# A planned one-layer kernel: new costs in the model of time of its planner, and a bound on how early a load is issued

## The chip, the cores and the metric

The kernel runs on one core of a Trainium2 chip. The metric is the device time of one execution in microseconds (us). The kernel before took 2209.79 us, the median of three runs that lie between 2207.43 and 2212.3. The execution that the profiler recorded took 2211.71 us; its span, from the first instruction to the last, is 2209.6 us.

The engines are PE (matrix multiplications), DVE, ACT and POOL (element by element) and SP, which here issues nearly all the DMAs. Each engine works through its own list of instructions in order.

## The reference

One layer of a streaming encoder, in fp32, for 1024 rows of width 1024 and 256 memory rows. Cut to what matters:

```python
h = rmsnorm(x, norm_mix_g)
p = h @ w_in                      # q, k, v, z, decay, beta | q, k, v, r, low-rank gate | two merge gates
# branch A, 8 heads of 128: gated delta rule in chunks of 64 rows
lower = where(strict, beta * (k k^T) * decay, 0)
sol = triangular_solve(I + lower, [beta * v, beta * exp(gc) * k])     # then a scan over the chunks
# branch B, 4 heads: gated linear attention (GLA) in chunks of 64 rows
x += merge(sigmoid gates, branch A @ w_bgdn, branch B @ w_bgla) @ w_out
x += cross_attention(rmsnorm(x), rmsnorm(mem))      # 4 heads over the 256 memory rows
x += w2 @ relu(w1 @ rmsnorm(x)) ** 2                # d_ff = 4096
out = rmsnorm(x)                                    # the final norm
```

## The kernel before

**The work.** All large products are done as three fp32r matmuls of split operands (mm3, L518): high by high (L525), high by low (L527), low by high (L529). A split (L563 to L566) is a copy by ACT, which gives the high part, and a subtraction by DVE or POOL, which gives the low part. Most products of 1024 by 1024 are further cut by a scheme of seven block products; its operands, in slots named A0a to B1b, are sums of blocks that are loaded (tiles e, raw, rawa), added and split.

**The stages**, in the order in which the program is written: a first phase that projects the memory's keys (units K0 to K3, 48 matmuls of 128x256 each) and folds them into the query weights (units Q0 to Q3, fold_q, results stored through the tile gst, L731), the same for the values (V0 to V3) and output weights (O0 to O3), and normalises x beside it; the gates (g0 to g3, the first users of the normalised x); GLA; the gated delta rule (GDN), four pairs of heads with a block inverse each; the merge; the output projection; attention; the MLP; the last norm. The weight loads of the first phase are named raw, two loads of 512 KB for a unit. In the names of the orders below, raw_389 and raw_395 are the two halves of K2's weights, raw_468 and raw_474 of K3's, raw_539 and raw_545 of Q0's. x comes in two halves of 512 rows (x_553, x_1044), each by four loads of 512 KB. x_norm (L747 to L758) sums the squares (L630 to L634 with colsum L608), takes a reciprocal root (L556 to L560), spreads it over the partitions by PE (L622), multiplies (L755) and splits the result (L758, L566) into the slots A0a to A1b. t_sums (L798 to L801) then forms block sums of x in place.

**GDN's inverse.** For a pair of heads, gdn_subst (L1262) solves blocks of 32 rows by a chain of 31 steps, a product (L1283) and a sum (L1285) each, between two STREAM_TRANSPOSE (L1276, L1289); gdn_inverse (L1309, L1318) combines the blocks by matmuls that need the chain's result (PF). The next heads' masks are made by gdn_decay (load L1194, then L1195 to L1203).

**What sets the order.** A class, Plan, records the whole program once, gives each instruction a cost and a latency (Op, L72), derives the dependences, and then makes each engine's list anew. latest (L276) goes backwards and gives each instruction the latest start at which PE still keeps its times. forward (L303) then simulates the engines: whenever one is free, it takes the ready instruction with the earliest latest start. In it "ring" is the DMA engines taken together, "port" a resource that DVE and POOL share, and work marked flex may go to either of them. Four rounds of this are made, and the best one's lists are what the program issues. So a changed cost can move instructions anywhere.

Of the kernel before, what the change touches and what calls it, by code (L numbers as in the profile page):

```python
# [13 lines left out]
AF = mybir.ActivationFunctionType  # L14
# [46 lines left out]
ENGINES = {mybir.EngineType.PE: "tensor", mybir.EngineType.DVE: "vector", mybir.EngineType.Activation: "scalar",  # L61
           mybir.EngineType.Pool: "gpsimd", mybir.EngineType.SP: "sync"}
GATES = (0, 1, 2, 3)
ROUNDS, TOP, PAD, WINDOW = 4, 228656, 128, 3413


def size(ap):
# [6 lines left out]
class Op:  # L74


    dma = port = False
    bytes = 0

    def __init__(self, ins, flex):  # L80
        eng = self.eng = ENGINES[ins.engine]
        ins_, outs = [[x for x in q if getattr(x, "bass_ap", None) is not None] for q in (ins.ins, ins.outs)]
        n = size(outs[0])
        psum = lambda x: x.bass_ap.tensor.name[:3] in ("pd_", "ps_")
        self.name, self.opcode, self.acc = ins.name, ins.opcode, []
        for w, q in enumerate((ins_, outs)):
            for x in q:
                p = x.ap[0][0]
                lows, span = [x.bass_ap.offset % p if p > 1 else x.bass_ap.offset], 0
                for st, k in sorted(x.ap[1:]):  # L90
                    if st <= span + 1 or k * len(lows) > 16:
                        span += st * (k - 1)
                    else:
                        lows = [lo + st * i for lo in lows for i in range(k)]
                for lo in lows:
                    self.acc.append((x.bass_ap.tensor.name,) + ((0, HALF) if psum(x) else (lo, lo + span)) + (w,))
        sums = ins.opcode == "TensorTensor"
        two = sum(size(x) > 1 and not psum(x) for x in ins_) > 1
        self.flex = flex and sums and two and n > 16
        scalar = n > 1 and any(size(x) == 1 for x in ins_)  # L100
        far = [x for x in ins_ + outs if not psum(x) and x.ap[-1][0] * 4 > 64]

        scan = 118 * (getattr(ins, "is_tensor_tensor_scan", None) or False)
        times = {"vector": (150 + scan + n * 1.042 + 60 * scalar, 85, 34, 35), "gpsimd": (290 + n * 1.98 if sums else 160 + n * 0.9, 45, 60, 35)}
        if sums and n <= 16:
            times["gpsimd"] = 430 + n * 152, 45, 60, 35
        if ins.opcode == "TensorReduce":
            times["vector"] = 420, 85, 34, 35
        if ins.opcode == "StreamTranspose":
            times["vector"] = 1880 if far else 1245, 85, 34, 35  # L110
        if ins.opcode == "Memset" and far:
            times["gpsimd"] = 450, 45, 60, 35
        self.times = {e: (d - early, early + own, early + lat) for e, (d, early, own, lat) in times.items()}
        if ins.opcode == "DMACopy":
            self.dma, self.cost, self.own, self.lat = True, 60, 2600, 2600
            self.bytes = n * 4 * outs[0].ap[0][1]
        elif eng == "tensor":
            m = size(ins_[0])
            if ins.is_transpose:
                self.cost = m * 0.85  # L120
            elif ins_[0].dtype == F32R:
                self.cost = m * 0.4463 + (4 if m < HALF else 0)
            elif m == 64:
                self.cost = 59
            else:
                self.cost = max(m, size(ins_[1])) * 1.667 + 8
            self.own, self.lat = 0, 203
        elif eng == "scalar":
            d = (150 if psum(ins_[0]) else 190) + n * 0.84 + 90 * scalar + n * 0.9 * bool(far)
            self.cost, self.own, self.lat = d - 100 + 240 * (len(outs) > 1), 130, 135  # L130
        else:
            self.port = eng == "gpsimd" or n > 16 and not any(psum(x) for x in ins_ + outs)
            self.take(eng)

    def take(self, eng):
# [9 lines left out]

class Mark:

    eng, port, dma, flex, acc, cost, lat, opcode, bytes = "mark", False, False, False, (), 0, 0, "", 0

    def to(self, other, raw):  # L150
        return 0
# [5 lines left out]
class Plan:  # L157
# [119 lines left out]
    def latest(self, deps, at, end):  # L277

        ops, n = self.ops, len(self.ops)
        last = [end] * n  # L280
        users, order = [0] * n, []
        for d in deps:
            for j in d:
                users[j] += 1
        todo = [i for i in range(n) if not users[i]]
        while todo:
            i = todo.pop()
            o = ops[i]
            s = last[i] = at[i] if o.eng == "tensor" else last[i] - o.cost
            for j in deps[i]:  # L290
                q = ops[j]
                if q.eng != "tensor":
                    last[j] = min(last[j], s - q.to(o, j in self.raw[i]) - q.bytes / 300)
                users[j] -= 1
                if not users[j]:
                    todo.append(j)
        return last

    def forward(self, deps, prio):


        ops, n = self.ops, len(self.ops)
# [7 lines left out]
        ready, start, work = [0.0] * n, [0.0] * n, defaultdict(float)  # L310
        engs = ("vector", "scalar", "gpsimd", "sync", "tensor")
        now_q = {e: [] for e in engs + ("flex",)}
        wait_q = {e: [] for e in engs + ("flex",)}
        free = dict.fromkeys(engs + ("port", "ring"), 0.0)
        order = {e: [] for e in engs}
        events = [0.0]

        def arrive(i):
            if ops[i].eng == "mark":
                start[i] = ready[i]  # L320
                return done(after[i], ready[i], None)
            heapq.heappush(wait_q["flex" if ops[i].flex else ops[i].eng], (ready[i], i))
            heapq.heappush(events, ready[i])

        def done(us, e, i):
            for u in us:
                ready[u] = max(ready[u], e + (0 if i is None else ops[i].to(ops[u], i in self.raw[u])))
                left[u] -= 1
                if not left[u]:
                    arrive(u)  # L330

        def run(i, t):
            o = ops[i]
            if o.port:
                t = max(t, free["port"])
                free["port"] = t + o.cost
            start[i], e = t, t + o.cost
            if o.eng == "tensor":

                k = int(t / WINDOW)  # L340
                if k and work[k - 1] < 0.4 * WINDOW:
                    e += o.cost
                work[k] += e - t
            free[o.eng] = e
            order[o.eng].append(i)
            heapq.heappush(events, e)
            if o.dma:
                e = free["ring"] = max(e, free["ring"]) + o.bytes / 300
            done(users[i], e, i)
            done(after[i], t, None)  # L350

# [24 lines left out]
        while events:  # L376
# [3 lines left out]
            for e in ("flex",) + engs:  # L380
                w = wait_q[e]
                while w and w[0][0] <= now:
                    i = heapq.heappop(w)[1]
                    heapq.heappush(now_q[e], (i if e == "tensor" else prio[i], i))
            for e in engs:
                if free[e] <= now:
                    i = take(e, now)
# [1988 lines left out]
```

## Time and profile before

| what | us |
|---|---|
| median of three runs | 2209.79 |
| lowest and highest run | 2207.43, 2212.3 |
| profiled execution | 2211.71 |
| its span | 2209.6 |
| PE busy in it | 2156.5 |
| DVE busy | 1702.4 |
| ACT busy | 1094.8 |
| POOL busy | 203.9 |

The mean granted clock of PE over the span is 0.991 of full speed. In the rows below, a stretch such as 21.40:47.40 is given in us from the span's start; "x127" counts instructions; the clock is the mean share of full speed that PE was granted in the stretch. Matmuls overlap, so their pitch (start to start) is shorter than the time of one. A wait "A <- B" means that A's engine stood idle until B ended.

### The profile page before, as it was taken

The page shows a single profiled execution, that of the slowest core. Times are in us where ns is not written, and L with a number is a line of the kernel's source. Part 1 is how long each engine was busy: PE and PEld are TensorE (multiplying, and loading weights), DVE is VectorE, ACT ScalarE, POOL GpSimd, SP SyncE. Part 2 cuts the span into 40 slices and gives each one's busy share as a digit, 9 for nine tenths or more (in the row PEclk, how much of TensorE's full clock was granted, in tenths as well). Part 3 has the DMA queues.
Part 4 walks back from the last instruction along what each step waited for, and adds up shares of the span by engine and source line. Part 5 has one row for each costly group of instructions (what it writes and reads, how often), then busy time and mean ns, then how long its engine had stood idle before and what let it go on. Part 6 is the DMA issues. An engine that isn't in the chain of part 4 may idle for free.

```text
span 2209.6 us, 32225 instructions
## 1 busy us (share of the span) xinstructions
PE 2156.5 (98%) x11504; PEld 1838.5 (83%) x11504; DVE 1702.4 (77%) x3167; ACT 1094.8 (50%) x2215; POOL 203.9 (9%) x236
## 2 busy tenths in 40 slices
PE   7999999999999999999999999999999999999996
PEld 7888988988888888888877888998788888888886
DVE  8935997878796887969769984569989778567756
ACT  6444555354454635555445343465665556544433
POOL 1100000000131321313010000000100000000001
PEclk8999999999999999999999999999999999999998
DMA  6942122221310211202077761345464446778742
GB/s 232 305 162 77 59 92 71 80 72 58 120 59 29 74 47 44 77 20 72 30 267 272 247 211 56 110 126 160 127 208 140 160 148 209 243 251 273 245 122 81
DMA packets 147312, 300.21 MB, mean 136 GB/s; under 512 B 15688, under 2 KB 22216, under 8 KB 147152
## 3 DMA queue, kind: packets, MB, share of 16 engines
q1 hardware_dynamic: 140352, 289.75, 39.7%
q10 hardware_dynamic: 6800, 8.42, 1.1%
q8 instruction: 90, 1.47, 0.3%
q14 instruction: 70, 0.57, 0.1%
HBM read 212.35 MB, written 85.75 MB: 135 GB/s over the span
## 4 chain that ended last, share of the span: by engine, by line
PE 77%; DVE 11%; DMA 4%; issue 2%; ACT 1%; POOL 0%; SPq 0%; DVEq 0%; POOLq 0%; ACTq 0%
PE pd L529 18%; PE pd L525 18%; PE pd L527 18%; PE ps L529 4%; PE ps L525 4%; PE ps L527 4%; PE ps L1318 1%; PE ps L597 1%; DVE wop L566 1%; DMA e<-obd 1%; PE ps L1309 1%; DVE pr L1283 1%; DVE Pm L1285 1%; DMA A0b<-tgd 1%; PE ps L1358 1%
## 5 line engine op out<-in xcount | busy, mean ns | idle before, releaser
L565 ACT ACTIVATE wop<-raw 128x512 fp32r<-128x512 f32 (+1 forms) x472 | 314.7, 672 | 496.2 <-PE pd L529 234.5
L566 DVE TENSOR_TENSOR wop<-raw,wop 128x512 fp32r<-128x512 f32 (+1 forms) x434 | 309.2, 715 | 133.3 <-ACT wop L565 126.9
L1176 DVE SCALAR_TENSOR_TENSOR acc<-pd,convw,acc 128x511 f32<-128x511 f32 x144 | 106.7, 741 | 19.3 <-ACT acc L1173 18.8
L529 PE MATMUL pd<-t,wop 128*128 128x512 f32 x268 | 107.7, 402 | 0.0
L525 PE MATMUL pd<-t,wop 128*128 128x512 f32 x268 | 105.8, 395 | 0.1
L527 PE MATMUL pd<-t,wop 128*128 128x512 f32 x268 | 105.3, 393 | 0.1
L525 PE MATMUL pd<-B1a,wop 128*128 128x512 f32 (+1 forms) x220 | 82.4, 375 | 0.3 <-ACT B1a L565 0.3
L529 PE MATMUL pd<-B1a,wop 128*128 128x512 f32 (+1 forms) x220 | 82.3, 374 | 0.0
L529 PE MATMUL pd<-A1a,wop 128*128 128x512 f32 x180 | 72.3, 402 | 0.0
L527 PE MATMUL pd<-A1a,wop 128*128 128x512 f32 x180 | 70.8, 393 | 0.6 <-DVE A1a L566 0.6
L525 PE MATMUL pd<-A1a,wop 128*128 128x512 f32 x180 | 70.9, 394 | 0.0
L527 PE MATMUL pd<-B0b,wop 128*128 128x512 f32 x172 | 67.0, 390 | 0.0
L565 ACT ACTIVATE whi<-raw 128x512 fp32r<-128x512 f32 x70 | 41.9, 625 | 38.7 <-PE pd L527 29.2
L527 PEld LDWEIGHTS pd<-t,wop 128*128 128x128 f32 x268 | 50.3, 188 | 12.2 <-DVE t L566 0.6
L529 PEld LDWEIGHTS pd<-t,wop 128*128 128x128 f32 x268 | 50.4, 188 | 11.7
L525 PEld LDWEIGHTS pd<-t,wop 128*128 128x128 f32 x268 | 50.4, 188 | 11.3 <-ACT t L565 0.5
L527 PE MATMUL pd<-B1a,wop 128*128 128x512 f32 (+1 forms) x156 | 57.5, 369 | 0.0
L529 PE MATMUL pd<-A1b,wop 128*128 128x512 f32 x144 | 56.9, 395 | 0.0
L525 PE MATMUL pd<-A1b,wop 128*128 128x512 f32 x144 | 56.9, 395 | 0.0
L525 PE MATMUL pd<-A0a,whi 128*128 128x512 f32 x140 | 55.8, 399 | 1.0 <-ACT whi L565 1.0
L527 PE MATMUL pd<-A1b,wop 128*128 128x512 f32 x144 | 56.4, 392 | 0.0
L529 PE MATMUL pd<-A0b,wlo 128*128 128x512 f32 x140 | 56.5, 403 | 0.0
(600 smaller groups left out, 6991.3 us busy)
## 6 DMA issues: line engine op xcount, KB each, us to landing
raw<-in_w_dram SPq DMA_DIRECT2D x120, 256.0 KB, 3.7
raw<-in_w_gdn_dram SPq DMA_DIRECT2D x64, 256.0 KB, 3.0
raw<-in_w_dram SPq DMA_DIRECT2D x32, 512.0 KB, 3.9
e<-ad SPq DMA_DIRECT2D x63, 256.0 KB, 4.8
ad<-q SPq DMA_DIRECT2D x45, 256.0 KB, 3.1
rawa<-ad SPq DMA_DIRECT2D x42, 256.0 KB, 4.8
A0b<-tgd SPq DMA_DIRECT2D x32, 256.0 KB, 5.0
ad<-acc SPq DMA_DIRECT2D x30, 256.0 KB, 2.4
```

Of the source, the lines that this page charges most:

```text
L525: nc.tensor.matmul(out, lh, rh, start=first and i == 0, stop=False)
L527: nc.tensor.matmul(out, lh, rl, start=False, stop=False)
L529: nc.tensor.matmul(out, ll, rh, start=False, stop=last and i == n - 1)
L565: nc.scalar.activation(hi, raw, AF.Copy)
L566: (lo_eng or nc.gpsimd).tensor_tensor(lo, raw, hi.bitcast(F32), SUB)
L597: self.nc.tensor.transpose(pt[:, i * P:(i + 1) * P], s, self.ident)
L1176: nc.vector.scalar_tensor_tensor(x, pt[:, 0:HALF - d], tap, x, MUL, ADD)
L1283: nc.vector.tensor_tensor(pr, X[:, c + 1:32, c:c + 1].broadcast_to([P, m, n]), Pm[:, c:c + 1, 0:n].broadcast_to([P, m, n]), MUL)
L1285: nc.vector.tensor_tensor(Pm[:, c + 1:32, 0:n], Pm[:, c + 1:32, 0:n], pr, ADD)
L1309: nc.tensor.matmul(pt[:, i * 96:(i + 1) * 96], NT[:, u + i, :], PF[:, v + i, 0:96], start=True, stop=True)
L1318: nc.tensor.matmul(pt[0:96, i * n:(i + 1) * n], PF[:, v + i, 0:96], Z, start=True, stop=True)
L1358: nc.tensor.matmul(py[:, 0:P], st["NT"][:, c, :], zh[h], start=True, stop=True)
```

## The change

The planner's numbers are changed, and one rule is added. A DMA is taken to need 2050 ns instead of 2600 ns beside its transfer, and the DMA engines to move 390 instead of 300 bytes in a ns. A matmul of 64 columns costs 80 instead of 59. A row sum (accum_out) by ACT from SBUF costs 385 instead of 240. ACT pays 1283 when the table of functions changes (Ln on one side, Exp and Tanh on the other). The shared port is also taken by small operations with two SBUF inputs. The rule: a DMA that writes a tile on the chip is not ready before 30,000 ns ahead of its latest start.

```diff
@@ -61,7 +61,7 @@
 ENGINES = {mybir.EngineType.PE: "tensor", mybir.EngineType.DVE: "vector", mybir.EngineType.Activation: "scalar",
            mybir.EngineType.Pool: "gpsimd", mybir.EngineType.SP: "sync"}
 GATES = (0, 1, 2, 3)
-ROUNDS, TOP, PAD, WINDOW = 4, 228656, 128, 3413
+ROUNDS, TOP, PAD, WINDOW, LOAD, HORIZON = 4, 228656, 128, 3413, 1283, 30000
 
 
 def size(ap):
@@ -75,6 +75,7 @@
 
 
     dma = port = False
+    table = 0
     bytes = 0
 
     def __init__(self, ins, flex):
@@ -112,7 +113,7 @@
             times["gpsimd"] = 450, 45, 60, 35
         self.times = {e: (d - early, early + own, early + lat) for e, (d, early, own, lat) in times.items()}
         if ins.opcode == "DMACopy":
-            self.dma, self.cost, self.own, self.lat = True, 60, 2600, 2600
+            self.dma, self.cost, self.own, self.lat = True, 60, 2050, 2050
             self.bytes = n * 4 * outs[0].ap[0][1]
         elif eng == "tensor":
             m = size(ins_[0])
@@ -121,15 +122,16 @@
             elif ins_[0].dtype == F32R:
                 self.cost = m * 0.4463 + (4 if m < HALF else 0)
             elif m == 64:
-                self.cost = 59
+                self.cost = 80
             else:
                 self.cost = max(m, size(ins_[1])) * 1.667 + 8
             self.own, self.lat = 0, 203
         elif eng == "scalar":
             d = (150 if psum(ins_[0]) else 190) + n * 0.84 + 90 * scalar + n * 0.9 * bool(far)
-            self.cost, self.own, self.lat = d - 100 + 240 * (len(outs) > 1), 130, 135
+            self.cost, self.own, self.lat = d - 100 + (240 if psum(ins_[0]) else 385) * (len(outs) > 1), 130, 135
+            self.table = {AF.Ln: 1, AF.Exp: 2, AF.Tanh: 2}.get(ins.func, 0)
         else:
-            self.port = eng == "gpsimd" or n > 16 and not any(psum(x) for x in ins_ + outs)
+            self.port = eng == "gpsimd" or (n > 16 or two) and not any(psum(x) for x in ins_ + outs)
             self.take(eng)
 
     def take(self, eng):
@@ -145,7 +147,7 @@
 
 class Mark:
 
-    eng, port, dma, flex, acc, cost, lat, opcode, bytes = "mark", False, False, False, (), 0, 0, "", 0
+    eng, port, dma, flex, acc, cost, lat, opcode, bytes, table = "mark", False, False, False, (), 0, 0, "", 0, 0
 
     def to(self, other, raw):
         return 0
@@ -290,7 +292,7 @@
             for j in deps[i]:
                 q = ops[j]
                 if q.eng != "tensor":
-                    last[j] = min(last[j], s - q.to(o, j in self.raw[i]) - q.bytes / 300)
+                    last[j] = min(last[j], s - q.to(o, j in self.raw[i]) - q.bytes / 390)
                 users[j] -= 1
                 if not users[j]:
                     todo.append(j)
@@ -311,7 +313,7 @@
         engs = ("vector", "scalar", "gpsimd", "sync", "tensor")
         now_q = {e: [] for e in engs + ("flex",)}
         wait_q = {e: [] for e in engs + ("flex",)}
-        free = dict.fromkeys(engs + ("port", "ring"), 0.0)
+        free = dict.fromkeys(engs + ("port", "ring", "table"), 0.0)
         order = {e: [] for e in engs}
         events = [0.0]
 
@@ -319,6 +321,9 @@
             if ops[i].eng == "mark":
                 start[i] = ready[i]
                 return done(after[i], ready[i], None)
+            if ops[i].dma and any(w and t in self.tiles for t, _, _, w in ops[i].acc):
+
+                ready[i] = max(ready[i], prio[i] - HORIZON)
             heapq.heappush(wait_q["flex" if ops[i].flex else ops[i].eng], (ready[i], i))
             heapq.heappush(events, ready[i])
 
@@ -334,6 +339,10 @@
             if o.port:
                 t = max(t, free["port"])
                 free["port"] = t + o.cost
+            if o.table:
+
+                t += LOAD * (o.table != free["table"])
+                free["table"] = o.table
             start[i], e = t, t + o.cost
             if o.eng == "tensor":
 
@@ -345,7 +354,7 @@
             order[o.eng].append(i)
             heapq.heappush(events, e)
             if o.dma:
-                e = free["ring"] = max(e, free["ring"]) + o.bytes / 300
+                e = free["ring"] = max(e, free["ring"]) + o.bytes / 390
             done(users[i], e, i)
             done(after[i], t, None)
```

The instructions are the same on SP and PE; their places differ, and some of the flex work changes its engine. From this line on, line numbers of the changed kernel are 9 higher than those of the kernel before (L494 is L503 there).

SP's list at the start, before (x_553 and x_1044 are the halves of x; raw_389 and raw_395 K2's weights):

```order
9 L494 DMA raw_323<-in_wk_dram 128x1024
10 L494 DMA raw_329<-in_wk_dram 128x1024
11 L494 DMA x_553<-in_xT_dram 128x2x512 x4
12 L494 DMA x_1044<-in_xT_dram 128x2x512 x4
13 L663 DMA convw_184<-in_convw_dram 128x96
14 L494 DMA raw_389<-in_wk_dram 128x1024
15 L494 DMA raw_395<-in_wk_dram 128x1024
16 L494 DMA raw_468<-in_wk_dram 128x1024
17 L494 DMA raw_474<-in_wk_dram 128x1024
18 L494 DMA raw_539<-in_wqT_dram 128x2x512
```

SP's list at the start, now:

```order
9 L503 DMA raw_323<-in_wk_dram 128x1024
10 L503 DMA raw_329<-in_wk_dram 128x1024
11 L503 DMA x_553<-in_xT_dram 128x2x512
12 L503 DMA raw_389<-in_wk_dram 128x1024
13 L503 DMA x_553<-in_xT_dram 128x2x512 x2
14 L503 DMA raw_395<-in_wk_dram 128x1024
15 L503 DMA x_553<-in_xT_dram 128x2x512
16 L503 DMA raw_468<-in_wk_dram 128x1024
17 L503 DMA raw_474<-in_wk_dram 128x1024
18 L503 DMA raw_539<-in_wqT_dram 128x2x512
...
30 L503 DMA raw_1055<-in_wv_dram 128x1024
31 L503 DMA x_1044<-in_xT_dram 128x2x512 x3
32 L503 DMA raw_1061<-in_wv_dram 128x1024
33 L503 DMA x_1044<-in_xT_dram 128x2x512
```

One load of x stands ahead of K2's first weight half and three ahead of its second; the loads of the second half of x stand behind those of Q0 to O0.

PE's list after K1, before (pd_336 is K1's second result, pd_401 K2's; ps tiles are the sums of squares and the spread roots of mem and x):

```order
97 L529 MATMUL pd_336<-mT_206,wlo_331 128x256
98 L622 MATMUL ps_480<-ident_171,rs_o_418 128x128 x2
99 L608 MATMUL ps_971<-ones_178,acc_704 128x1 x4
100 L622 MATMUL ps_1014<-ident_171,rs_o_980 128x128 x4
101 L608 MATMUL ps_1331<-ones_178,acc_1121 128x1 x2
102 L525 MATMUL pd_401<-mT_206,wop_390 128x256
103 L527 MATMUL pd_401<-mT_206,wop_390 128x256
104 L525 MATMUL pd_402<-mT_206,wop_390 128x256
105 L527 MATMUL pd_402<-mT_206,wop_390 128x256
```

PE's list after K1, now:

```order
96 L538 MATMUL pd_336<-mT_206,wlo_331 128x256
97 L534 MATMUL pd_401<-mT_206,wop_390 128x256
98 L536 MATMUL pd_401<-mT_206,wop_390 128x256
99 L538 MATMUL pd_401<-mT_206,wlo_391 128x256
100 L534 MATMUL pd_401<-mT_206,wop_390 128x256
101 L536 MATMUL pd_401<-mT_206,wop_390 128x256
102 L538 MATMUL pd_401<-mT_206,wlo_391 128x256
103 L534 MATMUL pd_401<-mT_206,wop_390 128x256
104 L536 MATMUL pd_401<-mT_206,wop_390 128x256
105 L617 MATMUL ps_411<-ones_178,acc_300 128x1 x2
106 L538 MATMUL pd_401<-mT_206,wlo_391 128x256
```

K1's last matmul is followed by K2's first; the memory's sum (ps_411) comes within K2. The sums and roots of x come in Q3, O0 and V3.

DVE's list in the second of GDN's substitutions, before (L1283 and L1285 are the chain, gl, kf and dm the next heads' masks, acc the convolution):

```order
1022 L1283 TENSOR_TENSOR pr_7303<-X_7274,Pm_7276 128x207
1023 L1185 SCALAR_TENSOR_TENSOR acc_7454<-tg_7496,acc_7454 128x512
1024 L1285 TENSOR_TENSOR Pm_7276<-Pm_7276,pr_7303 128x23x9
1025 L1195 COPY gl_7963<-dm_7961 128x8
1026 L1283 TENSOR_TENSOR pr_7306<-X_7274,Pm_7276 128x220
1027 L1202 TENSOR_TENSOR kf_7971<-gl_7963,tm_186 128x8
1028 L1285 TENSOR_TENSOR Pm_7276<-Pm_7276,pr_7306 128x22x10
...
1056 L1179 SCALAR_TENSOR_TENSOR acc_7618<-last_7619,convw_184,acc_7618 128x3
1057 L1198 TENSOR_TENSOR dm_7975<-dm_7975,tm_186 128x1024
1058 L1285 TENSOR_TENSOR Pm_7276<-Pm_7276,pr_7330 128x14x18
```

DVE's list at the same steps of the chain, now:

```order
1032 L1292 TENSOR_TENSOR pr_7306<-X_7274,Pm_7276 128x220
1033 L1294 TENSOR_TENSOR Pm_7276<-Pm_7276,pr_7306 128x22x10
1034 L1194 SCALAR_TENSOR_TENSOR acc_7618<-tg_7657,acc_7618 128x512
1035 L1292 TENSOR_TENSOR pr_7309<-X_7274,Pm_7276 128x231
1036 L1269 TENSOR_SCALAR eq_7616<-ssq_7589 128x8
1037 L1294 TENSOR_TENSOR Pm_7276<-Pm_7276,pr_7309 128x21x11
1038 L1292 TENSOR_TENSOR pr_7312<-X_7274,Pm_7276 128x240
1039 L1294 TENSOR_TENSOR Pm_7276<-Pm_7276,pr_7312 128x20x12
1040 L1292 TENSOR_TENSOR pr_7315<-X_7274,Pm_7276 128x247
...
1057 L1294 TENSOR_TENSOR Pm_7276<-Pm_7276,pr_7330 128x14x18
1058 L1292 TENSOR_TENSOR pr_7333<-X_7274,Pm_7276 128x247
```

L1195, L1198 and L1202 no longer stand between the steps; they come later, outside the substitution.

SP's list in the merge, before (obd and tgd are results of the branches in memory, A0a here a residual from xT):

```order
268 L494 DMA e_11364<-obd_71 128x512
269 L494 DMA e_11368<-obd_71 128x512
270 L494 DMA A0a_12276<-in_xT_dram 128x2x512 x4
271 L494 DMA A0b_11580<-tgd_109 128x512
272 L494 DMA A0b_11580<-tgd_108 128x512
273 L494 DMA A0b_11580<-tgd_110 128x512 x2
274 L494 DMA A0b_11580<-tgd_108 128x512
275 L494 DMA A0b_11580<-tgd_111 128x512
276 L494 DMA A0b_11580<-tgd_109 128x512
...
279 L494 DMA e_11372<-obd_71 128x512
280 L494 DMA rawa_11534<-obd_73 128x512
281 L494 DMA rawa_11538<-obd_73 128x512
```

SP's list in the merge, now:

```order
273 L503 DMA e_11372<-obd_71 128x512
...
275 L503 DMA e_11376<-obd_72 128x512
276 L503 DMA e_11381<-obd_72 128x512
277 L503 DMA rawa_11534<-obd_73 128x512
278 L503 DMA rawa_11538<-obd_73 128x512
...
280 L503 DMA e_11385<-obd_72 128x512
281 L503 DMA e_11389<-obd_72 128x512
282 L503 DMA e_11529<-obd_73 128x512
283 L503 DMA rawa_11555<-obd_74 128x512
284 L503 DMA rawa_11559<-obd_74 128x512
285 L503 DMA e_11542<-obd_73 128x512
...
296 L503 DMA A0b_11580<-tgd_109 128x512
```

The obd loads stand together and the A0b loads behind them; the four xT loads come at 413 to 427 of the list.

## Rows read from the trace of the kernel before

**Rows 1.** The page, part 1: engine, busy us (share of the span), xinstructions.

```profile
PE 2156.5 (98%) x11504; PEld 1838.5 (83%) x11504; DVE 1702.4 (77%) x3167; ACT 1094.8 (50%) x2215; POOL 203.9 (9%) x236
```

**Rows 2.** Windows: stretch, length, busy us (xinstructions) by engine, granted clock, DMA share, GB/s.

```profile
21.40:47.40 26.00, 19.28 (x127) 19.00 (x127) 21.60 (x35) 18.00 (x30) 8.27 (x6) 0.74 0.53 185
47.40:78.70 31.30, 25.30 (x202) 24.03 (x201) 29.06 (x51) 13.35 (x17) 4.41 (x3) 1.00 0.78 246
78.70:130.30 51.60, 51.58 (x313) 45.06 (x314) 37.91 (x52) 29.46 (x42) 2.21 (x1) 1.00 0.92 314
...
552.40:1104.80 552.40, 542.09 (x3190) 471.53 (x3188) 443.50 (x1050) 280.61 (x797) 126.30 (x167) 0.99 0.18 57
1104.80:1215.30 110.50, 105.86 (x484) 84.57 (x483) 89.39 (x154) 54.55 (x108) 6.79 (x4) 1.00 0.78 269
```

**Rows 3.** Waits of PE: what waited, releaser, us in total, times, longest.

```profile
PE ps L1309 <- ACT PF L1295: 6.4, 3, 2.6
PE pd L525 <- DVE gst L731: 5.3, 4, 1.7
...
PE ps L1309 <- issue: 2.8, 1, 2.8
PE ps L525 <- ACT B1b L565: 2.8, 3, 1.4
```

**Rows 4.** Timeline of PE: start, us, instruction, idle before it and releaser.

```profile
30.05 2.08 PE L622 MATMUL ps<-ident,rs_o 128*128 128x128 f32 x8 [4.20 <-DVE rs_o L560]
...
47.25 0.28 PE L529 MATMUL pd<-mT,wlo 128*128 128x256 f32 x1
47.37 0.28 PE L525 MATMUL pd<-kv,wop 128*128 128x256 f32 x1
```

**Rows 5.** DMA, 0 to 36 us: rate by slice, issues, us to landing.

```profile
GB/s 0 0 130 341 314 328 266 325 241 314 394 337 416 394 394 403 396 385 389 387 389 385 391 378 391 377 405 397 423 387 382 118 32 0 0 0 0 0 0 46
...
x<-in_xT_dram SPq DMA_DIRECT2D x8, 512.0 KB, 9.4
raw<-in_wk_dram SPq DMA_DIRECT2D x6, 512.0 KB, 10.3
```

**Rows 6.** Timeline of ACT: the copy of K2's first weight half.

```profile
27.59 1.04 ACT L565 ACTIVATE wop<-raw 128x1024 fp32r<-128x1024 f32 x1
```

**Rows 7.** Groups of DVE instructions by form, 21.4 to 78.7 us.

```profile
L566 DVE TENSOR_TENSOR wlo<-raw,wop 128x1024 fp32r<-128x1024 f32 x13 | 18.0, 1385 | 2.0 <-PE pd L529 1.7 <-issue 0.2
L755 DVE SCALAR_TENSOR_TENSOR x<-x,cols,ps 128x512 f32<-128x512 f32 x14 | 9.9, 736 | 0.8 <-PE ps L622 0.8
L731 DVE TENSOR_TENSOR gst<-pd,rmb 128x256 f32<-128x256 f32 x26 | 9.6, 413 | 1.8 <-DMA Gd<-gst 1.7
L634 DVE TENSOR_TENSOR acc<-acc,sq 128x512 f32<-128x512 f32 x11 | 7.6, 692 | 0.6
```

**Rows 8.** Groups of POOL instructions by form, 6.5 to 80 us.

```profile
L566 POOL TENSOR_TENSOR A1a<-x,A1a 128x512 fp32r<-128x512 f32 x2 | 3.5, 1748 | 7.0 <-ACT A1a L565 7.0
```

**Rows 9.** Groups of DVE instructions by form, 78.7 to 130.3 us.

```profile
L798 DVE TENSOR_TENSOR x<-x 128x512 f32<-128x512 f32 x4 | 2.6, 686 | 0.0
```

**Rows 10.** Timeline of PE around 130 us: first use of row half 1.

```profile
130.26 0.40 PE L525 MATMUL pd<-A1b,wop 128*128 128x512 f32 x1
```

**Rows 11.** Timeline of PE in GDN, the first inverse.

```profile
674.12 6.89 PE L1309 MATMUL ps<-PF,NT 128*128 128x96 f32 x32 [2.82 <-issue]
```

**Rows 12.** Groups of DVE instructions in GDN, 631 to 672 us.

```profile
L1176 DVE SCALAR_TENSOR_TENSOR acc<-pd,convw,acc 128x511 f32<-128x511 f32 (+2 forms) x9 | 6.7, 741 | 0.6 <-ACT acc L1173 0.6
```

**Rows 13.** DMA of 1104.8 to 1165 us: issues, KB each, median us to landing.

```profile
e<-obd SPq DMA_DIRECT2D x18, 256.0 KB, 5.1
...
A0a<-in_xT_dram SPq DMA_DIRECT2D x4, 512.0 KB, 9.1
```

**Rows 14.** The page, part 6: DMA issues, KB each, median us to landing.

```profile
e<-ad SPq DMA_DIRECT2D x63, 256.0 KB, 4.8
...
rawa<-ad SPq DMA_DIRECT2D x42, 256.0 KB, 4.8
```

## The prediction

> **What bounds the kernel now.** I read the busy shares first, then the stretches, PE's waits, and the timeline inside the stretches that lose time. PE is busy 2156.5 of 2209.6 us [rows 1], so a change that issues the same instructions can win only where PE stands still or runs slowly. Three places do so. From 21.4 to 47.4 us PE is busy 19.28 of 26.00 us at a mean granted clock of 0.74, from 47.4 to 78.7 us 25.30 of 31.30; in GDN 10.3 of 552.4 us are idle, in the merge 4.6 of 110.5 [rows 2]. The longest waits belong to the same places: L1309 waits for the block inverses, fold_q for gst, the merge's matmuls for split operands [rows 3]. In the rest of the span matmul follows matmul, and a shifted load or split can win nothing there; it can only lose.
>
> **The start: -16.** The first loss is a queue. SP issues all eight 512 KB loads of x ahead of K2's weights. The ring then moves 385 to 400 GB/s [rows 5], so a load of 512 KB takes 1.36 us of it; the x loads need 9.4 us to land, the wk loads 10.3, and ACT can copy K2's first half only at 27.59 [rows 6]. Meanwhile PE does the sums of x and stands still 4.20 us before 30.05 [rows 4]; 0.26 of the clock is missing in 26 us, which is some 13 us at the 1.2 GHz level.
> The change leaves one x load ahead of raw_389 (K2's first half) and three ahead of raw_395. They land 7 x 1.36 = 9.5 and 5 x 1.36 = 6.8 us earlier, the first near 17, the second near 20 to 21. A half then needs an ACT copy (1.04) and a DVE subtraction (1.22 alone, 1.39 on average [rows 7]). So K2 follows K1 at 21.4; its second half is wanted 24 matmuls later and I allow 1.5 us of waiting. K2 and K3 are 96 matmuls of 128x256; PE starts one every 0.12 us [rows 4], less a little: 11.0 us. With 1 us for the memory's sums, Q0 begins at 21.4 + 11.0 + 1.5 + 1 = 34.9 and not at 47.37: 12.5 us gained.
> The Q stage is held by DVE. A weight half is 24 matmuls, 2.75 us of PE, and one subtraction and four gst, 1.22 + 4 x 0.41 = 2.86 us of DVE. Before, x_norm's multiplications and some splits stood between them (29.06 us of DVE in 31.30). Now DVE's order has 32 gst, 8 subtractions and one small rsqrt there, 23.7 us: I put V0 at 34.9 + 24.5 = 59.4, and not at 78.7.
> What left comes back later. Between Q3 and the first matmul on row half 1 DVE now has 16 multiplications of L755 (0.74), 16 weight subtractions, 8 kv (0.42), 7 sums (0.69) and 14 splits of x (0.68, 6 of them POOL's before): 11.8 + 19.5 + 3.4 + 4.8 + 9.5 + 0.8 = 49.8 us. The 16 operations of t_sums (0.69 each [rows 9]) stood in this stretch and go behind the splits. PE's own work there is the 51.6 us of [rows 2] plus some 2 us for the colsums and rows moved in. I take 54. The first matmul on half 1 then stands at 113.4, not at 130.26 [rows 10]: 16.9 earlier, of which I keep 16, because DVE is full 0.92 of the time. Bounds: all PE idles and slow clock of 21.4 to 78.7 gone, 25; nothing but the early Q0 minus a DVE that falls behind, 5.
> A row bears on the six splits: POOL needs 1.75 us for one [rows 8], and beside POOL DVE's subtraction averages 1.39 against 1.22. Thirteen of them lose 13 x 0.17 = 2.2 us, so the move costs DVE 6 x 0.68 = 4.1 and returns up to 2.2; I count the 4.1 whole. The Trainium skill (SBUF — State Buffer, "Who interferes with whom") says that a DVE operation with two SBUF inputs and a GpSimd operation that reads SBUF exclude each other for the whole instruction. The slower mean agrees with it; by that rule alone the stage would be 2 us shorter.
>
> **GDN: -6.** L1309 waits four times for the block inverse, 6.4 + 2.8 = 9.2 us [rows 3], and the first run after such a pause takes 6.89 us for 32 matmuls [rows 11]. The mean clock of 0.99 over 552 us is some 5 us more. The inverse is a chain of 31 steps on DVE (L1283, L1285), and other DVE work stands between them: in the 41 us that end at the first inverse, nine conv steps of 0.74 alone take 6.7 us [rows 12]. DVE's order shows the next head's mask arithmetic (L1195, L1198 and L1202) out of the second and third substitution, because the load that it starts from may no longer come early. Counted by order, the foreign DVE work falls from 27.8 to 21.9 us, 27.9 to 21.9 and 22.8 to 21.8 in the second to fourth; in the first by 1.9, but there L1309 also stands 13 rows earlier in PE's order (13 x 0.227 = 3 us), which eats it. So I take nothing from the first, 2.6 + 2.4 + 1.4 (the waits for PF) from the others, where in the fourth L1309 also stands 22 rows later and 1.7 of the clock: 8.1, of which 6 are kept since up to six chain steps go to POOL, slower than DVE. Bounds 0 and 14. The mask work comes back outside the chain, where DVE is busy 0.80 of the time.
>
> **Merge: -4.** Here PE idles 4.6 us, 2.8 of it for ACT's copy of obd operands [rows 3], and ring time decides again: four xT loads (512 KB, 9.1 us to land) and eight A0b loads stand ahead of obd loads [rows 13], 4.2 MB or 11 us of ring at 385 GB/s, though the xT data is used after 1310. Behind them the obd operands come first: the wait goes. The xT loads issue some 150 us later, each between two weight loads. Bounds 0 and -6.
>
> **What may be lost: +3.** 105 operand loads of the MLP [rows 14] and the other loads may no longer run far ahead. The plan holds a load until 30 us before its latest start; it needs 4.8 us from issue to landing, 9 to 10 on a full ring, so most have room. In the merge 18 obd loads cost PE some 3.5 us, 0.19 us a load. I take a tenth of that rate for 137 loads, 2.6, and round up; bounds 0 and 26. The renewed costs (table loads, row sums, 64-wide matmuls) shift ACT and PE entries by a place or two; no row shows what one such place costs, the nearest is a wait of PE that one late entry made, 2.8 us at most [rows 3], so -3 to +3; I take 0, since PE's order in the MLP is as before.
>
> **Sum.** -16 - 6 - 4 + 3 = -23. The profiled execution took 2211.7 us, 2.1 more than its span, and stands 1.9 above the median of the runs. 2211.7 - 23 = 2188.7 for it, 2187 against the median.
>
> **Rivals.**
> DVE takes PE's place. In the V/O stage 49.8 of 54 us of DVE is a chain of short operations that wait for ACT copies and PE. For it: DVE stood 0.93 busy in the Q stage before and PE waited on gst 5.3 us. Against it: x_norm's operations have slack until half 1 is used. If each of the 16 L755 with its split is paid on the path, 16 x (0.74 + 0.68) = 23 us of DVE with half of it uncovered, 11 us go back: 2187 + 11 = 2198.
> The loads come too late. Mechanism: SP's queue is in order, so a load held back to its last 30 us stands behind a DMA that still waits for its buffer; ACT's copy, DVE's split and every later split behind it wait too, and after a pause PE runs at the lower clock, as in [rows 2]. With the merge's 0.19 us for each of 137 loads (32 A0b, 63 e, 42 rawa) that is 26 us, plus about 5 us of clock as in GDN: 2187 - 3 + 31 = 2215, slower. It decides from 0.2 us a load. For it: the ring is busy 0.78 in the merge. Against: 30 us are three times the slowest landing in the rows (10.3), and the plan knows the ring. The Trainium skill (DMA: Bandwidth & Descriptors, "Anatomy of one DMA") says that DMA engines do not wait on semaphores, the issuing sequencer does, before dispatch; by that every load behind a waiting one is late by the same time. No row here shows such a chain in the MLP.
> Only the order of idle work changes. PE's waits are gaps between the plan and the chip, and new ones open where old ones close. For it: 98% of the span is matmul. Against: K2's weights came late by seven loads of 1.36 us, which order alone decides. It gives 2209.
> All waits vanish: start -25, GDN -12, merge -5, nothing lost: 2210 - 42 = 2168.
>
> **Chances.** Forecast 0.56 (its own range 2177 to 2196), DVE as bound 0.18, loads too late 0.10, order only 0.08, all waits gone 0.08. What differs by under 0.2% (4.4 us) a measurement here hardly tells from no change. Faster means below 2205.4: the forecast, nearly all of the DVE case and the last, 0.82; same takes the middle of "order only", 0.08; slower 0.10. The range 2168 to 2210 leaves out the late loads and the rest of the tails.
>
> **What will show it.** Right: the copy of K2's first half near 17 us, Q0 near 35, V0 near 59, the first use of half 1 near 114; a granted clock near 1.00 from 21 to 47; waits for PF below 4 us; no wait on B1b in the merge. Wrong, and how: Q0 early but half 1 not before 122 means DVE as bound; new PE waits on ACT or DVE splits released by e<-ad, rawa<-ad or A0a<-in_xT after 1216 mean late loads; an unchanged idle sum means order only.

## The result

The changed kernel takes 2213.9 us (median of 20 runs, 2209.02 to 2219.38), the kernel before 2210.6 (20 runs, 2203.68 to 2213.29): a ratio of 1.002 with an interval of 1.0012 to 1.0028, so slower by 0.2%. Forecast were 2187. The recorded execution took 2218.4 us, 4.5 above its median, with a span of 2216.6.

The stretches of the changed kernel that answer to [rows 2], and two behind them (stretch, length, busy us by engine, granted clock, DMA share, GB/s):

```profile
21.40:47.40 26.00, 24.53 (x208) 24.35 (x208) 20.11 (x37) 13.43 (x19) 0.71 (x1) 1.00 0.73 230
47.40:78.70 31.30, 24.80 (x167) 22.23 (x166) 19.57 (x39) 12.48 (x19) 1.01 (x1) 0.95 0.94 309
78.70:130.30 51.60, 49.36 (x282) 42.54 (x281) 43.39 (x64) 34.00 (x53) 4.70 (x3) 0.97 0.66 215
...
552.40:1104.80 552.40, 548.77 (x3265) 477.61 (x3264) 442.66 (x1059) 286.70 (x823) 131.52 (x174) 1.00 0.17 59
1104.80:1215.30 110.50, 107.94 (x481) 88.54 (x480) 94.76 (x153) 53.92 (x93) 10.30 (x7) 1.00 0.73 248
1215.30:1325.80 110.50, 104.31 (x431) 81.28 (x431) 89.25 (x143) 39.04 (x68) 1.63 (x1) 0.97 0.69 241
1325.80:2154.40 828.60, 819.13 (x3989) 687.79 (x3988) 604.59 (x1019) 418.20 (x751) 25.44 (x17) 0.99 0.53 171
```

The last two of them in the kernel before:

```profile
1215.30:1325.80 110.50, 110.27 (x483) 90.26 (x482) 98.51 (x161) 44.59 (x76) 1.47 (x1) 1.00 0.67 229
1325.80:2154.40 828.60, 828.04 (x4059) 698.46 (x4058) 605.68 (x1027) 422.49 (x757) 24.54 (x16) 1.00 0.53 172
```

PE works earlier in the first stretch, and it idles 3.6 us in GDN against 10.3, and 2.6 in the merge against 4.6. Then come losses that the kernel before does not have: 6.2 us idle from 1215 to 1326 (0.2 before), with 0.03 of the clock, and 9.5 from 1326 to 2154 (0.6 before). Most of PE's waits are new ones; the one for gst is old, 4.6 us against 5.3 (compare [rows 3]):

```profile
...
PE pd L534 <- ACT kv L724: 5.4, 3, 3.3
PE pd L534 <- DVE u L1723: 5.3, 5, 2.0
PE pd L534 <- DVE gst L740: 4.6, 4, 1.5
PE pd L534 <- ACT wop L574: 4.2, 4, 2.6
PE pd L538 <- DVE wop L575: 3.6, 4, 2.3
PE pd L534 <- ACT B0a L574: 2.8, 1, 2.8
...
PE ps L1318 <- ACT PF L1304: 2.4, 3, 0.9
```

PF, the inverse's wait, falls from 9.2 us (with "issue") to 2.4. In its place stand waits for copies, subtractions and sums of operands (kv, u, wop, B0a).

To compare kernels I sum, over neighbouring matmuls, the time from start to start less the pitch of their shape in calm stretches (0.227 us for 128x512, 0.1145 for 128x256, and so on). This lost time of PE holds waits and low clock alike. By stretch, in us (e5 and e6 are experiments that follow below):

| kernel | 0-110 | 110-552 | GDN 552-1105 | merge 1105-1215 | 1215-1326 | 1326-2099 | from 2099 |
|---|---|---|---|---|---|---|---|
| before | 25.3 | 27.4 | 24.4 | 8.5 | 1.2 | 6.7 | 7.7 |
| changed | 21.7 | 29.0 | 12.7 | 3.5 | 13.0 | 16.9 | 12.9 |
| bound alone (e5) | 18.3 | 27.4 | 15.1 | 1.9 | 0.5 | 6.9 | 10.1 |
| DMA numbers alone (e6) | 25.4 | 27.2 | 26.0 | 6.4 | 11.5 | 23.8 | 11.1 |

From the first two rows: 3.6 + 11.7 + 5.0 us are won up to 1215, 1.6 are lost from 110 to 552 and 27.2 after 1215. The difference is 8.5, less 1.1 because the first matmul starts earlier; the spans differ by 7.0. The recorded execution is a long one, 4.5 us above its median. In e4 below, where by the traces PE's order differs in 15 of 11504 places and ACT's in 9 of 2215, the recorded execution stands 1.3 above the median and 21.7 us more than before are lost after 1215. So some 5 of the 27.2, most of them near 2125, belong to this one execution.

How one such loss comes about, from the changed kernel's ACT (timeline) ahead of PE's longest wait between 1215 and 1326:

```profile
1266.29 0.63 ACT L574 ACTIVATE B0a<-e 128x512 fp32r<-128x512 f32 x1 [6.24 <-DMA e<-md]
...
1291.43 0.63 ACT L574 ACTIVATE B1a<-q 128x512 fp32r<-128x512 f32 x1 [3.74 <-DVE q L1824]
...
1293.83 0.63 ACT L574 ACTIVATE B0a<-u 128x512 fp32r<-128x512 f32 x1 [0.57 <-DVE u L1824]
```

and from PE behind it:

```profile
1294.52 0.80 PE L534 MATMUL pd<-B0a,wop 128*128 128x512 f32 x1 [2.82 <-ACT B0a L574]
...
1296.26 0.80 PE L536 MATMUL pd<-B0b,wop 128*128 128x512 f32 x1 [0.95 <-DVE B0b L575]
```

ACT waits for a loaded operand, then for DVE's sums of others; its list is in order, so each late arrival moves all that is behind it, and PE meets it once its lead is used up. After the pause of 2.82 us PE's granted clock is 0.50 from 1294.50 to 1300.00, its lower level of 1.2 GHz (0.94 from 1290.00 to 1294.50); the two matmuls take 0.80 us, those ahead of the pause 0.39. The chain of waits that ends at 1296.26 goes back over DVE's sums to a load of A0b:

```profile
1280.94 1.96 DMA A0b<-tgd
...
1284.79 0.07 DVE q L1681
...
1293.71 0.69 DVE u L1823
1294.40 0.60 DVE B1b L575
1295.00 0.60 DVE u L1824
1295.60 0.61 DVE B0b L575
```

### The profile page after: what moved, and what is told of

It is laid out like the page before. It is cut to its first block, busy times and chain, and to the rows that moved or that the text cites. A ratio compares the mean times of both kernels' runs of the same rounds, so it can differ in the third digit from the quotient of the medians.

```text
span 2216.6 us, 32151 instructions
## 1 busy us (share of the span) xinstructions
PE 2160.5 (97%) x11504; PEld 1835.2 (83%) x11504; DVE 1702.1 (77%) x3161; ACT 1092.8 (49%) x2215; POOL 208.2 (9%) x242
## 4 chain that ended last, share of the span: by engine, by line
PE 71%; DMA 11%; DVE 11%; ACT 2%; issue 2%; SPq 1%; POOL 0%; DVEq 0%; ACTq 0%; POOLq 0%
PE pd L538 18%; PE pd L534 18%; PE pd L536 18%; DMA raw<-in_w_dram 3%; PE ps L534 2%; PE ps L538 2%; PE ps L536 2%; DVE wop L575 2%; PE ps L606 1%; DMA e<-ad 1%; PE ps L1327 1%; DMA Gd<-gst 1%; SPq L503 1%; DMA A0b<-tgd 1%; DMA rawa<-pd 1%
## 5 line engine op out<-in xcount | busy, mean ns | idle before, releaser
L534 PEld LDWEIGHTS pd<-t,wop 128*128 128x128 f32 x268 | 50.4, 188 | 12.7 <-ACT wop L574 2.0
L536 PEld LDWEIGHTS pd<-t,wop 128*128 128x128 f32 x268 | 50.4, 188 | 11.6
L538 PE MATMUL pd<-A1a,wlo 128*128 128x512 f32 x140 | 56.3, 402 | 0.0
```

The source lines that it names most:

```text
L534: nc.tensor.matmul(out, lh, rh, start=first and i == 0, stop=False)
L536: nc.tensor.matmul(out, lh, rl, start=False, stop=False)
L538: nc.tensor.matmul(out, ll, rh, start=False, stop=last and i == n - 1)
```

## The experiments

Three theories of the losses were put against each other, and a fourth (D) for the gains. A: the bound of 30 us makes loads late. B: the renewed DMA numbers let the plan believe in transfers faster than the chip's. C: any shift of the numbers moves the stalls about by chance. D, for the gains: they come from the other costs (tables, row sums, 64-wide matmuls, port). Each edit is to the changed kernel unless said otherwise.

| run | us (range) | ratio to before, interval |
|---|---|---|
| e1 no bound | 2238.42 (2233.85-2240.92) | 1.0124, 1.0106-1.0143 |
| e2 old DMA numbers | 2192.0 (2190.57-2192.62) | 0.9916, 0.9902-0.993 |
| e3 bound for x only | 2228.12 (2226.45-2235.82) | 1.008, 1.0065-1.0094 |
| e4 2060 ns | 2213.49 (2209.47-2216.13, and one run of 4370.14) | 1.0012, 1.0002-1.0022 |
| e5 before + bound | 2192.43 (2188.98-2192.6) | 0.9916, 0.9904-0.9929 |
| e6 before + DMA numbers | 2237.42 (2235.21-2241.28) | 1.0121, 1.0105-1.0137 |
| e7 300 bytes per ns | 2202.92 (2199.26-2204.21) | 0.9966, 0.9954-0.9978 |
| e8 2600 ns | 2213.49 (2208.61-2215.89) | 1.0011, 1.0001-1.002 |
| e9 2600 ns, 340 | 2200.43 (2199.13-2202.47) | 0.9955, 0.9942-0.9968 |
| e10 2600 ns, 260 | 2220.34 (2218.28-2222.93) | 1.0045, 1.0033-1.0057 |
| e11 2600 ns, 300 backward, 390 forward | 2213.44 (2206.0-2218.15) | 1.0009, 0.9998-1.0021 |
| e12 2600 ns, 390 backward, 300 forward | 2191.65 (2190.26-2193.33) | 0.9916, 0.9903-0.9929 |

**e1, the bound away.**

```diff
-ROUNDS, TOP, PAD, WINDOW, LOAD, HORIZON = 4, 228656, 128, 3413, 1283, 30000
+ROUNDS, TOP, PAD, WINDOW, LOAD, HORIZON = 4, 228656, 128, 3413, 1283, 10000000
```

> The changed kernel with the bound of 30 us on loads taken away (10 ms in its place); all renewed costs stay. Theory A (the bound makes loads late): the stalls of the changed kernel after 1215 us, some 27 us of PE beyond its pitch against 15 before, go back to 15; but the x loads stand ahead of K2's weights again, so the start loses its 4 us and the merge its 8; near 2205 to 2210. Theory B (the renewed DMA numbers, 2050 ns and 390 bytes per ns, let the plan place loads later than the chip carries them): the stalls after 1215 us stay; near 2222. Theory C (any shift of the plan's numbers moves stalls about by chance): stalls in new places, anywhere in 2200 to 2225.

28 us slower than before. A falls: the bound does not cost, it gains, and the losses after 1215 stay without it (10.6 and 21.6 us).

**e2, the old DMA numbers.**

```diff
-            self.dma, self.cost, self.own, self.lat = True, 60, 2050, 2050
+            self.dma, self.cost, self.own, self.lat = True, 60, 2600, 2600
...
-                    last[j] = min(last[j], s - q.to(o, j in self.raw[i]) - q.bytes / 390)
+                    last[j] = min(last[j], s - q.to(o, j in self.raw[i]) - q.bytes / 300)
...
-                e = free["ring"] = max(e, free["ring"]) + o.bytes / 390
+                e = free["ring"] = max(e, free["ring"]) + o.bytes / 300
```

> The changed kernel with the old DMA numbers (2600 ns, 300 bytes per ns); the bound and the other renewed costs stay. A: the loads stay late, since 30 us are counted from the latest start; stalls after 1215 us stay above 20 us, 2210 to 2214. B: the latest starts lie earlier by 0.55 us and 0.4 to 0.8 us of transfer per load and the simulated ring is slower, so the stalls after 1215 us fall to 15 or less and the early gains stay: near 2195. C: stalls in new places.

B, and 18 us faster than before. The stretch 1215 to 1326 of this run, beside that of the changed kernel above:

```profile
1215.30:1325.80 110.50, 110.50 (x486) 90.64 (x485) 90.11 (x147) 41.88 (x70) 0.00 (x0) 1.00 0.64 225
```

PE idles 0.0 us, with 486 matmuls instead of 431. In the changed kernel ACT's largest wait there is for a weight load; it is gone here, and ACT waits for PE to free buffers (the changed kernel, then e2, both from 1215.3 to 1294):

```profile
ACT wop L574 <- DMA raw<-in_w_bgdn_dram: 9.2, 2, 5.8
```

```profile
ACT wop L574 <- PE pd L538: 15.9, 9, 2.2
ACT wop L574 <- PE ps L538: 15.1, 8, 2.1
```

**e3, the bound for loads of x only.**

```diff
-            if ops[i].dma and any(w and t in self.tiles for t, _, _, w in ops[i].acc):
+            if ops[i].dma and any("in_xT" in t for t, _, _, w in ops[i].acc if not w):
```

> The changed kernel with the bound kept for loads of x (in_xT) alone, so for 16 of several hundred loads. A: K2's weights still come early, and the merge's obd loads too, while w2, weight and operand loads run ahead again: stalls after 1215 us near 15, the start as in the changed kernel or better: 2195 to 2202. B: the stalls after 1215 us stay, 2212 or more. C: new places.

B again. With 390 bytes per ns the loads of x alone bring 10 of the 25 us that lie between e1 and the changed kernel.

**e4, a change that means nothing.**

```diff
-            self.dma, self.cost, self.own, self.lat = True, 60, 2050, 2050
+            self.dma, self.cost, self.own, self.lat = True, 60, 2060, 2060
```

> The changed kernel with 2060 instead of 2050 ns for a DMA, a difference that means nothing by itself. A and B: the same stalls as in the changed kernel, within 2 us of it (2212 to 2216). C: stalls at other places and a time that differs from the changed kernel's by more than 4 us.

Within 0.4 us of the changed kernel and with losses in the same stretches (11.6 from 1215 to 1326, 16.7 to 2099). So C falls for so small a step; for larger ones it is answered by the rates tried below.

**e5, before and the bound alone**: the rule of the diff put into the kernel before, with HORIZON = 30000, no number changed.

> The kernel before with the bound of 30 us added and no number changed. Theory B (the DMA numbers make loads late, the bound gains): K2 early, stalls after 1215 us no more than before's 15, so 2190 to 2198, like the run with the old DMA numbers. Theory A (the bound costs): 2210 or more. Theory D (the other renewed costs, of table loads, row sums and 64-wide matmuls, carry the gain of that run): near 2205.

B; D falls, since the other costs are not in this kernel and it is as fast as e2.

**e6, before and the DMA numbers alone**: 2050, 2050 and 390 for 2600, 2600 and 300.

> The kernel before with the renewed DMA numbers (2050 ns, 390 bytes per ns) and nothing else. B: the stalls after 1215 us rise to 25 or more and nothing gains at the start: 2225 to 2240. A: no loss, within 4 us of before. D: as A.

B. With e1, e2 and e5 this closes a square: the bound takes off 18 us at the old numbers and 24 at the new ones, the numbers add 27 without the bound and 22 with it. The other renewed costs do nothing that shows: 2192.0 with them, 2192.43 without, and 2238.42 against 2237.42.

**e7 and e8, which of the two numbers.**

```diff
-                    last[j] = min(last[j], s - q.to(o, j in self.raw[i]) - q.bytes / 390)
+                    last[j] = min(last[j], s - q.to(o, j in self.raw[i]) - q.bytes / 300)
...
-                e = free["ring"] = max(e, free["ring"]) + o.bytes / 390
+                e = free["ring"] = max(e, free["ring"]) + o.bytes / 300
```

> The changed kernel with 300 instead of 390 bytes per ns; 2050 ns and the bound stay. B has two halves. If the simulated rate of all DMAs together is what makes loads late, this run comes near the run with both old numbers, 2190 to 2198; if it is the fixed 550 ns, it stays near 2210.

```diff
-            self.dma, self.cost, self.own, self.lat = True, 60, 2050, 2050
+            self.dma, self.cost, self.own, self.lat = True, 60, 2600, 2600
```

> The changed kernel with 2600 instead of 2050 ns; 390 bytes per ns and the bound stay. If the fixed 550 ns make loads late, 2190 to 2198; if the rate does, near 2210; if both halves are needed, this run and the one with 300 bytes per ns both lie between, 2198 to 2206.

The rate: 300 brings 11 us and clears 1215 to 1326 (0.3 us lost), 2600 ns alone brings nothing (13.4 lost there). Neither fits its line wholly: at 300 the fixed 550 ns are worth another 11, mostly at the start and the end.

**e9 and e10, more rates**, both with 2600 ns; the diff is that of e2 with 340 or 260 for 300.

> The changed kernel with 2600 ns and 340 bytes per ns. The windows of the trace move 315 to 345 GB/s per busy share of 1.00 outside the first 20 us, so a plan that assumes 340 still believes in slightly more than the chip gives in the poorer stretches. Theory B (a rate above that of the busy stretches makes loads late): between the run with 300 (2192) and the one with 390 (2213), near 2198, with 1215 to 1326 us at most half of the 13 us lost at 390. Theory C (chance of the list): no order by rate, anywhere in 2190 to 2240.

As B says: between 300 and 390, with 6.3 us lost from 1215 to 1326.

> The changed kernel with 2600 ns and 260 bytes per ns, below every busy stretch. B: no new stalls from late loads, 2188 to 2196; a plan too careful may lose some of the start's gain. C: anywhere in 2190 to 2240.

Missed. 260 is worse than 300 by 28 us. The start has 33.2 us lost there, and SP's list puts all four loads of x's first half ahead of K2's weights, and PE waits for the root of a sum before K2:

```profile
24.22 1.19 PE L631 MATMUL ps<-ident,rs_o 128*128 128x128 f32 x4 [3.23 <-DVE rs_o L569]
```

and 1215 to 1326 loses 8.4. So time is not simply better the more careful the plan is; why 260 orders the start so was not followed up. The 8.4 us are not late loads either: ACT's idle time that a DMA ended is 2.5 us there, and PE's longest wait, 4.4 us, is for a subtraction of DVE.

**e11 and e12, where the rate acts**, both with 2600 ns.

```diff
-                    last[j] = min(last[j], s - q.to(o, j in self.raw[i]) - q.bytes / 390)
+                    last[j] = min(last[j], s - q.to(o, j in self.raw[i]) - q.bytes / 300)
```

> The changed kernel with 2600 ns, 300 bytes per ns in the backward pass (the latest starts) and 390 in the forward simulation of the DMA engines. B by the latest starts: the bound and the priorities are right again, 2190 to 2198. B by the simulated engines: the forward pass still lets ACT and DVE queue up behind loads that it believes landed, 2208 to 2216.

```diff
-                e = free["ring"] = max(e, free["ring"]) + o.bytes / 390
+                e = free["ring"] = max(e, free["ring"]) + o.bytes / 300
```

> The changed kernel with 2600 ns, 390 bytes per ns in the backward pass and 300 in the forward simulation. B by the latest starts: loads get their priority 0.2 to 0.4 us later each, stalls stay, 2208 to 2216. B by the simulated engines: the order of ACT, DVE and SP again fits what lands when, 2190 to 2198.

The whole 22 us hang on the forward simulation. With 390 there, 2213.44 (e11) and 2213.49 (e8), whatever the latest starts; with 300, 2191.65 and 2192.0 (e2). So it is not that loads get too low a priority. e12, e2 and e5 are the fastest of all, 2191.65 to 2192.43, and beat both kernels.

The times of e11 and e8 agree, but not the places. PE's lost time in the four kernels with 2600 ns, in us:

| simulated rate, rate of the latest starts | GDN | merge | 1215-1326 | 1326-2099 | from 2099 |
|---|---|---|---|---|---|
| 300, 300 (e2) | 14.1 | 3.6 | 0.7 | 9.3 | 7.6 |
| 300, 390 (e12) | 14.5 | 5.1 | 2.9 | 7.7 | 7.5 |
| 390, 300 (e11) | 21.9 | 6.2 | 10.8 | 9.7 | 10.4 |
| 390, 390 (e8) | 15.0 | 2.4 | 13.4 | 15.8 | 9.1 |

From 1215 to 1326 the loss goes with the simulated rate. Why e11 loses more in GDN, and e8 more after 1326, is open; that both come to 2213 may be chance in part.

That late loads make this loss is read from ACT's waits from 1215.3 to 1325.8. Its idle time that a DMA ended sums to 23.1 us in the changed kernel and to 25.3 to 35.8 in the other six at a simulated 390, with the bound or without it (e1, e3, e4, e6, e8, e11); to 17.1 at 340 (e9); and to 0.7 to 7.7 in the five at 300 (before, e2, e5, e7, e12). PE loses 10.6 to 15.3, 6.3, and 0.3 to 2.9 us there. So the lists of ACT, DVE and SP are made for arrivals that the chip does not keep, and for this stretch C falls too. After 1326 the two do not go together so well: e7 loses 9.2 us of PE there with 122.6 of such waits of ACT (1326 to 2154), the changed kernel 16.9 with 155.4, e1 21.6 with 73.8. Which late arrivals cost PE there is open.

## Why the prediction was wrong

**The step that failed is "What may be lost: +3".** It priced the later stages by the bound ("most have room") and took a tenth of the merge's rate of loss. From 1215 us on 27.2 us were lost in the recorded execution and 21.7 in e4's, so about the upper bound of 26. The bound was not the cause (e1, e5): a forward simulation at 390 bytes per ns was (e12). The sum has no term for the two DMA numbers; against late loads the prediction said that "the plan knows the ring". 390 agrees with the 385 to 400 GB/s of the loads at the start [rows 5], and what the DMA engines move elsewhere was not asked. With +3 there the changed kernel would have come to about 2190 to 2195; e2, e5 and e12 did, at 2191.65 to 2192.43. The rows were there: 314 GB/s at a DMA share of 0.92, 269 at 0.78 and 246 at 0.78 [rows 2] are 341, 345 and 315 for a full ring. For a 256 KB operand alone on the ring the new numbers give 2.05 + 0.67 = 2.7 us, the old ones 2.6 + 0.87 = 3.5; the trace has 4.8, queueing on the ring included [rows 14]. The change went away from it. That these rates are why 300 fits is argued from them and from e9, not shown apart; e10 says that the relation does not go on below 300.

**The rival "the loads come too late"** had the place, the clock and nearly the time (2215 against 2213.9), with a chance of 0.10. Its sign came in part: ACT's copies wait for e<-ad in the MLP, though PE's own waits there are mostly for a sum of DVE (u, 5.3 us). From 1325.8 to 2154.4, the largest group of ACT's waits for e<-ad before, then now:

```profile
ACT A1a L565 <- DMA e<-ad: 2.5, 2, 1.4
```

```profile
ACT A1a L574 <- DMA e<-ad: 18.1, 7, 6.7
```

It had the wrong cause: loads held back by the bound. All of ACT's waits for e<-ad and rawa<-ad there sum to 13.2 us before, 37.4 with the DMA numbers alone (e6), 57.2 with the bound alone (e5) and 121.5 with both, so the bound does take ACT's lead away; but PE's lost time from 1326 to 2099 is 6.7, 23.8, 6.9 and 16.9, and goes with the numbers. In e12 most of it goes, though the bound is there and its latest starts are reckoned at 390. That 2215 came so near is luck in part: the rival kept 26 us of gains and lost 31, and some 19 and 22 to 27 were measured.

**The rival "only the order of idle work changes"** said 2209 and has its sign nearly too: PE stands idle 56.1 us of the span against 53.1. But two effects that cancel are not an unchanged sum: alone the bound takes 18 us off (e5), and alone the numbers add 27 (e6).

**The start, -16: right to 61 us, then mis-sized.** ACT copies K2's first half at 16.16 (17 was said), Q0 begins at 32.23 (34.9), V0 at 61.34 (59.4). Half 1 is first used at 125.14, and not at 113.4.

ACT's copy, and then the PE rows of these moments (timelines):

```profile
16.16 1.05 ACT L574 ACTIVATE wop<-raw 128x1024 fp32r<-128x1024 f32 x1
```

```profile
32.23 0.28 PE L534 MATMUL pd<-kv,wop 128*128 128x256 f32 x1
...
70.88 0.49 PE L534 MATMUL pd<-wop,kv 128*128 128x512 f32 x1 [3.32 <-ACT kv L724]
...
125.14 0.40 PE L534 MATMUL pd<-A1b,wop 128*128 128x512 f32 x1
```

I had made DVE the limit of the stage. Between Q0 and V0 DVE is busy 19.03 of 29.10 us, the ring 0.85 (window, columns as above):

```profile
32.20:61.30 29.10, 24.54 (x202) 23.86 (x201) 19.03 (x36) 8.76 (x9) 0.73 (x1) 1.00 0.85 258
```

DVE waits for the ring, which must take the stores of gst before their buffers come free (waits in that window):

```profile
DVE gst L740 <- DMA Gd<-gst: 7.9, 4, 3.1
```

From V0 to the first use of half 1 pass 63.8 us, not 54: PE idles 5.7 of them, at a granted clock of 0.95. DVE is busy 49.83 of them, as summed (49.8). So the prediction's own sign of DVE as bound came (half 1 after 122), but not its mechanism: DVE has 14 us free. The longest of PE's waits, 3.32 us before 70.88, is for a copy of kv, and the chain behind it goes over ACT's list back to DVE and to a store of gst (chain of waits, to 71):

```profile
60.46 7.77 DMA Gd<-gst
...
68.59 0.43 DVE gst L740
...
69.04 0.33 ACTq L741
...
69.41 0.25 ACT acc L639
...
70.56 0.28 ACT kv L724
...
70.88 0.49 PE pd L534
```

A store of 256 KB takes 2.05 + 0.67 = 2.7 us by the new numbers; this one stands in the chain with 7.77. ACT issues the next store, then does work of x, and the copy of kv stands behind them in its list. From 47.4 to 78.7 us (0.94 of the ring, 309 GB/s) the DMA issues are (KB each, median us to landing):

```profile
Gd<-gst ACTq DMA_DIRECT2D x10, 256.0 KB, 5.8
...
raw<-in_wo_dram SPq DMA_DIRECT2D x4, 512.0 KB, 5.3
x<-in_xT_dram SPq DMA_DIRECT2D x4, 512.0 KB, 7.4
```

So 3.6 us of 16 remain in the changed kernel, and 8.1 in e12, the best there of the three fastest kernels: even at the rate of 300 half of the term was not to be had.

**GDN, -6: right in kind, too small.** 11.7 us were gained. The first inverse, from which I took nothing, no longer waits either: PE has no wait between 660 and 690 us, and its clock is 1.00 in GDN (0.99 before); the waits for PF are the 2.4 us above. e1 and e6, without the bound, lose 24.9 and 26.0 there, e5 15.1: the bound does it. The mechanism was right, and it holds for the first inverse too. Before, the mask operations stood within each of the first three chains, from the first L1283 to the last L1285, and these took 40.8, 41.7 and 41.4 us; now they take 34.3, 34.6 and 34.6 without them. The fourth had none in either kernel, 35.0 and 34.6. In e3, where the bound does not hold the mask's load, masks stay in the first three chains (38.6 to 40.7 us) and 17.4 us are lost. In the first chain before, one of the mask operations and the last step:

```profile
640.28 2.04 POOL L1198 TENSOR_TENSOR dm<-dm,tm 128x1024 f32<-128x1024 f32 x1
...
667.02 0.25 POOL L1285 TENSOR_TENSOR Pm<-Pm,pr 128x31 f32<-128x31 f32 x1 [4.45 <-DVE pr L1283]
```

Now, its last step and the same kind of mask operation, which comes 48 us behind it:

```profile
655.41 0.18 DVE L1294 TENSOR_TENSOR Pm<-Pm,pr 128x31 f32<-128x31 f32 x1
...
703.76 1.23 DVE L1207 TENSOR_TENSOR dm<-dm,tm 128x1024 f32<-128x1024 f32 x1
```

**The merge, -4: right.** 5.0 us gained, and there is no wait on B1b; e5 (1.9 lost) and e1 (8.7) put that to the bound too.

**The other costs, 0: right** (e2 against e5, e1 against e6).

## What to carry to other kernels

When a change mixes a rule and new numbers in a planner, price each alone: here a good rule of 18 us hid behind numbers that cost 22 to 27. A rate measured where one kind of load streams undisturbed was too high for a plan of mixed traffic: divide the GB/s of the busy stretches by their DMA share, and look at the landing times of the operand loads. Here that gives 315 to 345, and of the rates tried 300 was best, 340 and 260 worse; so try the rates below that figure too. And an in-order list made for arrivals that come too late loses twice, by the wait and by the clock after it.

## What was not expected of the hardware

With the opening loads alone the ring held 390 GB/s for 18 us (10 to 28 us, kernel before). From 47.4 to 78.7 us of the changed kernel, with stores of gst among the loads, it moved 309 at a DMA share of 0.94, and single slices of 0.8 us there lay between 42 and 419.
